# Background stages of the mixers: one at every product instead of at set distances

## The chip, the cores and the metric

The kernel runs on one core of a Trainium2 chip. The metric is the device time of one execution in microseconds (us). Three runs of the kernel before gave 865.61, 866.16 and 866.32 us; the median is 866.16 us.

## What is computed

Two layers of a streaming encoder over 256 positions of 1024 features, in float32. Cut to what matters here, a layer is:

```python
mod = cond @ ada_w[l] + ada_b[l]              # sh1, sc1, g1, sh2, sc2, g2
h = rmsnorm(x, norm1_g[l]) * (1 + sc1) + sh1
proj = h @ w_in + b_in                        # 1024 -> 6733: all q, k, v and gates
o_a = dsa_attention(...)      # 6 heads; top 64 keys of a query by an indexer of 8 heads
o_b = chunk_band_attention(...)               # 5 heads, relative bias
o_c = forgetting_attention(...)               # 5 heads, cumulated log forget gate
y = g0*(o_a @ wb_a) + g1*(o_b @ wb_b) + g2*(o_c @ wb_c)     # sigmoid gates
x = x + g1 * (y @ w_out)
h = rmsnorm(x, norm2_g[l]) * (1 + sc2) + sh2
x = x + g2 * ((silu(h @ w_g) * (h @ w_u)) @ w_ffn_out)
```

A last RMSNorm follows. A head has 64 features; softmax is taken over the 256 keys.

## The kernel before

**Products.** Every large matrix product runs in three passes: a weight is split into a rounded part `whi` (ScalarE, L187) and a rest `wlo` (VectorE, L188), the activations into `hT` of two parts, and TensorE adds hi·hi, hi·lo and lo·hi in one PSUM bank. Weights come in pieces (two blocks of 128 rows); six are held, and a piece is made when one has been used up. The 15 blocks of the input projection, the branch products and the output projection follow each other on TensorE as one stream, the *foreground*.

**Background.** All other work of the mixers is written as Python generators whose `yield` marks the end of a stage: `evac` (bias, rotary, transposes to head-major form, L560), `idx_pair` and `topk` (indexer and selection, L692 and L693 on VectorE), `forget`, and `pair`, which does two heads of an attention branch (one head for the fifth of B and C). `pair` has three stages: the scores of both heads (float32 products with 64 rows of the array each, so that two heads lie side by side: L648, L650), with VectorE taking logits and maxima (L772) and ScalarE the exponentials and the division (L776, L780); then the transposes of the weights on TensorE (L785) with their copies out of PSUM (L786); then the products with v (L792, 64 columns of the array for each of two heads, 128 for a single one). Two pairs are active at a time (`WINDOW`), so mostly four heads go through together, the *double block*; branches B, C and A follow each other. A layer has three double blocks, two single heads and one last pair.

**Order.** After each foreground product the code calls `beat(ns)`, which advances a clock by the product's nominal length (642 for six 256-column products) and then runs one stage of every generator whose time has come. The time is the clock at the last stage plus what the generator yielded: 7000 ns after the scores, 1500 after the transposes, 12000 before the rows of the gates g1 and g2 are transposed (L355, in `ada_mac`), 1500 between steps of the selection. This makes the program order. It is not the order on the engines: a list scheduler goes over the program with estimated durations and, on each engine, takes the earliest written instruction that it holds ready. Each engine then runs its own list strictly in order and waits on semaphores. PSUM has four banks for the foreground (`ps_g`) and four for the background (`ps_x`); a bank is given out again when its readers are done.

Of the kernel before, what the change touches and what calls it, by code (L numbers as in the profile page):

```python
# [94 lines left out]
def hybrid_encoder(ctx: ExitStack, tc: tile.TileContext, a):  # L95
# [105 lines left out]
    def get():  # L201
        while not ready:
            pump(1)
            if not ready:
                advance(urgent)
        got[0] += 1
        return ready.pop(0)
# [6 lines left out]

    WINDOW, LG_BUFS = 2, 4
    SKIP0, SKIP1 = 14, 22
    clock = [0.0]
    queue, active, urgent, aside = [], [], [], []  # L220

    def advance(gens):
        for e in list(gens):
            if clock[0] >= e[1]:
                try:
                    e[1] = clock[0] + next(e[0])
                except StopIteration:
                    gens.remove(e)

    def beat(ns):  # L230
        clock[0] += ns
        advance(urgent)
        advance(aside)
        while len(active) < WINDOW and queue and not (queue[0] is None and active):
            g = queue.pop(0)
            if g is not None:
                active.append([g, clock[0]])
        advance(active)
# [938 lines left out]
```

## Time and profile before

| | |
|---|---|
| median of three runs | 866.16 us |
| the profiled execution | 866.67 us, span 864.9 us |
| TensorE busy | 839.1 us (97%) |
| VectorE busy | 643.0 us (74%) |
| ScalarE busy | 473.8 us (55%) |
| granted TensorE clock | 0.997 |

The span is the time from the first to the last instruction. The mixer of the first layer takes the stretch from about 74 to 196 us, that of the second from about 470 to 606 us. In the timeline a row gives the start, the time that the row covers, engine, line, operation and count; since products overlap in the array, their cost is read from the starts of successive rows, not from their durations.

### The profile page before, as it was taken

What the parts mean: (1) busy time and instruction counts of PE and PEld (TensorE: products, weight loads), DVE (VectorE), ACT (ScalarE), POOL (GpSimd) and SP (SyncE); (2) the same over time, 40 slices, a digit from 0 to 9 for tenths busy, and PEclk for the clock granted to TensorE, in tenths of its full rate; (3) what the DMA queues carried; (4) which work ended last, traced back from release to release, by engine and by line L of the source; (5) the groups of instructions that cost most, each with busy time, mean ns of one, the idle gap of its engine ahead of it and who ended that gap; (6) DMA issues with size and microseconds to landing.
All of it is one profiled execution on the core that took longest, in us unless ns stands there. A gap on an engine that the chain in (4) does not pass through costs nothing.

```text
span 864.9 us, 14940 instructions
## 1 busy us (share of the span) xinstructions
PE 839.1 (97%) x5918; PEld 779.4 (90%) x5918; DVE 643.0 (74%) x1106; ACT 473.8 (55%) x795; POOL 51.5 (6%) x91
## 2 busy tenths in 40 slices
PE   2999999999999999999999999999999999999996
PEld 2999998999988999998889999898998899999886
DVE  6986897969987776698475786787898755647734
ACT  5556866764564544365255576767456544445521
POOL 2011210000010000000012013000000100000001
PEclk9999999999999999999999999999999999999999
DMA  9967566668846776589354456477795566636801
GB/s 353 414 251 240 186 223 225 230 232 342 316 154 274 253 273 230 184 335 380 138 194 126 142 192 240 147 280 259 272 372 194 202 222 223 218 118 255 321 14 49
DMA packets 32437, 200.48 MB, mean 232 GB/s; under 512 B 3872, under 2 KB 4144, under 8 KB 13680
## 3 DMA queue, kind: packets, MB, share of 16 engines
q1 hardware_dynamic: 30672, 194.77, 61.4%
q0 software_dynamic: 1264, 4.38, 1.6%
q8 instruction: 46, 0.75, 0.4%
q10 hardware_dynamic: 432, 0.39, 0.1%
q14 instruction: 23, 0.19, 0.1%
HBM read 198.48 MB, written 1.05 MB: 231 GB/s over the span
## 4 chain that ended last, share of the span: by engine, by line
PE 84%; DVE 9%; DMA 3%; issue 2%; ACT 2%; POOL 0%; POOLq 0%; DVEq 0%
PE ps_g L452 15%; PE ps_g L454 14%; PE ps_g L453 14%; PE ps_g L316 11%; PE ps_g L317 11%; PE ps_g L318 11%; DVE wlo L188 3%; DMA raw<-in_ada_w_dram 2%; DVE raw L340 2%; PE ps_x L650 1%; PE ps_x L454 1%; PE ps_x L452 1%; PE ps_x L453 1%; PE ps_x L792 1%; PE ps_x L648 1%
## 5 line engine op out<-in xcount | busy, mean ns | idle before, releaser
L188 DVE TENSOR_TENSOR wlo<-raw,whi 128x1024 fp32r<-128x1024 f32 (+5 forms) x300 | 333.6, 1128 | 132.6 <-ACT whi L187 131.6
L187 ACT ACTIVATE whi<-raw 128x1024 fp32r<-128x1024 f32 (+5 forms) x300 | 288.3, 975 | 248.5 <-PE ps_g L453 133.7
L452 PE MATMUL ps_g<-hT,whi 128*128 128x256 f32 x1056 | 302.2, 286 | 0.0
L454 PE MATMUL ps_g<-hT,wlo 128*128 128x256 f32 x1056 | 298.5, 283 | 0.0
L453 PE MATMUL ps_g<-hT,whi 128*128 128x256 f32 x1056 | 297.6, 282 | 0.0
L452 PEld LDWEIGHTS ps_g<-hT,whi 128*128 128x128 f32 x1056 | 199.3, 189 | 3.8 <-issue 3.7
L453 PEld LDWEIGHTS ps_g<-hT,whi 128*128 128x128 f32 x1056 | 199.5, 189 | 0.4 <-issue 0.3
L454 PEld LDWEIGHTS ps_g<-hT,wlo 128*128 128x128 f32 x1056 | 199.0, 188 | 0.3 <-issue 0.3
L340 DVE CUSTOM_DVE_ANT_0 raw<-raw,cond,adab 128x1024 f32<-128x1024 f32 x96 | 122.8, 1299 | 21.4 <-DMA raw<-in_ada_w_dram 21.2
L316 PE MATMUL ps_g<-whi,hT 128*128 128x512 f32 (+4 forms) x320 | 118.3, 372 | 1.2 <-ACT hT L1048 1.2
L317 PE MATMUL ps_g<-wlo,hT 128*128 128x512 f32 (+4 forms) x320 | 117.3, 367 | 1.8 <-DVE wlo L188 1.8
L318 PE MATMUL ps_g<-whi,hT 128*128 128x512 f32 (+4 forms) x320 | 116.6, 366 | 0.0
L316 PEld LDWEIGHTS ps_g<-whi,hT 128*128 128x128 f32 x320 | 60.5, 190 | 11.1 <-issue 2.3
L317 PEld LDWEIGHTS ps_g<-wlo,hT 128*128 128x128 f32 x320 | 60.6, 189 | 9.5 <-DVE wlo L188 2.0
L318 PEld LDWEIGHTS ps_g<-whi,hT 128*128 128x128 f32 x320 | 60.7, 190 | 7.9
L316 PE MATMUL ps_g<-whi,aT 128*128 128x512 f32 (+1 forms) x176 | 66.4, 377 | 0.0
L317 PE MATMUL ps_g<-wlo,aT 128*128 128x512 f32 (+1 forms) x176 | 66.3, 377 | 0.0
L318 PE MATMUL ps_g<-whi,aT 128*128 128x512 f32 (+1 forms) x176 | 66.2, 376 | 0.0
L380 POOL TENSOR_SCALAR var<-sq 128x1 f32<-128x1 f32 x9 | 6.2, 694 | 600.8 <-ACT xn L378 598.2
L776 ACT ACTIVATE lg<-lg,mx 128x128 f32<-128x128 f32 x64 | 28.3, 443 | 20.1 <-DVE mx L772 20.0
L316 PEld LDWEIGHTS ps_g<-whi,aT 128*128 128x128 f32 x176 | 33.1, 188 | 6.0
L318 PEld LDWEIGHTS ps_g<-whi,aT 128*128 128x128 f32 x176 | 33.1, 188 | 6.1
(212 smaller groups left out, 956.4 us busy)
## 6 DMA issues: line engine op xcount, KB each, us to landing
raw<-in_ada_w_dram SPq DMA_DIRECT2D x48, 1024.0 KB, 5.3
raw<-in_w_ffn_in_dram SPq DMA_DIRECT2D x40, 1024.0 KB, 4.9
raw<-in_w_in_dram SPq DMA_DIRECT2D x30, 1024.0 KB, 5.3
raw<-in_w_ffn_out_dram SPq DMA_DIRECT2D x20, 1024.0 KB, 6.4
raw<-in_w_branch_dram SPq DMA_DIRECT2D x12, 768.0 KB, 4.6
raw<-in_w_in_dram SPq DMA_DIRECT2D x16, 512.0 KB, 8.7
raw<-in_w_out_dram SPq DMA_DIRECT2D x8, 1024.0 KB, 6.4
raw<-in_w_in_dram SPq DMA_DIRECT2D x8, 768.0 KB, 4.6
```

The lines of the kernel that those rows point to most:

```text
L187: nc.scalar.activation(hi, r, AF.Copy)
L188: nc.vector.tensor_sub(lo, r, hi.bitcast(F32))
L316: nc.tensor.matmul(ps, lh, wh, start=start, stop=False)
L317: nc.tensor.matmul(ps, lh, wl, start=False, stop=False)
L318: nc.tensor.matmul(ps, ll, wh, start=False, stop=stop)
L340: nc.vector.tensor_tensor_reduce(out=wj, in0=wj, in1=cond, op0=OP.mult, op1=OP.add, scale=ngain[:, l, int(name[2]) - 1, k:k + 1] if name[: ...
L452: nc.tensor.matmul(ps, wh[:, c], ah, start=first, stop=False, skip_group_check=True)
L453: nc.tensor.matmul(ps, wh[:, c], al, start=False, stop=False, skip_group_check=True)
L454: nc.tensor.matmul(ps, wl[:, c], ah, start=False, stop=stop, skip_group_check=True)
L648: nc.tensor.matmul(p[:, 0:P], q[:, 0:P], k[:, 0:P], start=True, stop=True)
L650: nc.tensor.matmul(p[:, P:3 * P], q[:, P:S], k, start=True, stop=True)
L776: nc.scalar.activation(lg[:, REG[t]], lg[:, REG[t]], AF.Exp, bias=mx[:, t:t + 1], scale=-1.0, accum_out=sm[:, t:t + 1])
```

## The change

A generator's time is no longer moved on by what it yields. The delay with which a generator is started (`spawn(e, d)`, so the 7000 to 10000 before the first transposes of `evac`) stays; all later distances are gone, and each active generator runs one stage at every `beat`. The scheduler, the pools, the work itself and the loads are the same.

```diff
@@ def advance(gens):
         for e in list(gens):
             if clock[0] >= e[1]:
                 try:
-                    e[1] = clock[0] + next(e[0])
+                    next(e[0])
                 except StopIteration:
                     gens.remove(e)
```

An empty line is added above, so lines after 217 have a number one higher in the new kernel.

On TensorE, in the first layer's double block of branch B: the products with v (64x256 and 64x128; `lg` the weights of a head, `ps_x` the bank written). Before:

```order
L318 MATMUL ps_g_1200<-whi_1066,hT1_109 128x384
L792 MATMUL ps_x_1280<-lg_1086,v_vb_907 64x256
L792 MATMUL ps_x_1280<-lg_1087,v_vb_907 64x256
L792 MATMUL ps_x_1280<-lg_1086,v_vb_907 64x128
L792 MATMUL ps_x_1280<-lg_1087,v_vb_907 64x128
L792 MATMUL ps_x_1287<-lg_1112,v_vb_907 64x256
L792 MATMUL ps_x_1287<-lg_1113,v_vb_907 64x256
L792 MATMUL ps_x_1287<-lg_1112,v_vb_907 64x128
L792 MATMUL ps_x_1287<-lg_1113,v_vb_907 64x128
```

And now, at the same place (L786 the transposes of the fourth head, L649 and L651 the scores of the fifth):

```order
L786 MATMUL ps_x_1120<-ident_87,lg_1068 128x128
L793 MATMUL ps_x_1154<-lg_1041,v_vb_907 64x256
L786 MATMUL ps_x_1120<-ident_87,lg_1068 128x128 x2
L793 MATMUL ps_x_1154<-lg_1042,v_vb_907 64x256
L793 MATMUL ps_x_1154<-lg_1041,v_vb_907 64x128
L793 MATMUL ps_x_1154<-lg_1042,v_vb_907 64x128
L793 MATMUL ps_x_1161<-lg_1067,v_vb_907 64x256
L649 MATMUL ps_x_1181<-f4_0_814 128x128
L651 MATMUL ps_x_1181<-f4_0_814 128x256
L793 MATMUL ps_x_1161<-lg_1068,v_vb_907 64x256
L793 MATMUL ps_x_1161<-lg_1067,v_vb_907 64x128
L793 MATMUL ps_x_1161<-lg_1068,v_vb_907 64x128
```

The products of two heads that stood next to each other are parted by transposes and by the scores of another head.

On ScalarE, ahead of the same double block: the first softmax of the layer. Before, the forget gate (`fa`) came ahead of it, with two loads of an activation table:

```order
L721 ACT_TABLE_LOAD
L721 ACTIVATE fa_1336<-fa_1336 128x10
L187 ACTIVATE whi_1138<-raw_860 128x768
L722 ACT_TABLE_LOAD
L722 ACTIVATE fa_1336<-fa_1336 128x10
L776 ACT_TABLE_LOAD
L776 ACTIVATE lg_1086,sm_1095<-lg_1086,mx_1094 128x128
L776 ACTIVATE lg_1086,sm_1095<-lg_1086,mx_1094 128x256
```

And now:

```order
L187 ACTIVATE whi_1000<-raw_778 128x768
L187 ACTIVATE whi_1023<-raw_812 128x768
L777 ACT_TABLE_LOAD
L777 ACTIVATE lg_1041,sm_1050<-lg_1041,mx_1049 128x128
L777 ACTIVATE lg_1041,sm_1050<-lg_1041,mx_1049 128x256
L777 ACTIVATE lg_1042,sm_1059<-lg_1042,mx_1058 128x128
L781 ACTIVATE lg_1041<-lg_1041,sm_1050 128x128
L781 ACTIVATE lg_1041<-lg_1041,sm_1050 128x256
L777 ACTIVATE lg_1042,sm_1059<-lg_1042,mx_1058 128x256
```

The softmax stands ahead of the forget gate, with one table load (which here waits for the maxima of VectorE), and a head is divided as soon as its exponentials are done.

## Rows read from the trace of the kernel before

**Rows 1.** The page: busy us, share of the span and instructions of each engine.
```profile
PE 839.1 (97%) x5918; PEld 779.4 (90%) x5918; DVE 643.0 (74%) x1106; ACT 473.8 (55%) x795; POOL 51.5 (6%) x91
```

**Rows 2.** Windows of the two mixers: length, busy PE, PEld, DVE, ACT, POOL.
```profile
74.00:196.00 122.00, 120.23 (x937) 111.87 (x937) 100.50 (x254) 85.80 (x197) 10.95 (x18) 1.00 0.62 224
470.00:606.00 136.00, 135.29 (x1062) 127.32 (x1061) 101.86 (x256) 93.59 (x212) 10.07 (x16) 1.00 0.60 207
```

**Rows 3.** Timeline, TensorE: products with v of two pairs, foreground around.
```profile
146.85 0.28 PE L826 MATMUL ps_g<-oh,whi 128*128 128x256 f32 x1
146.97 0.29 PE L827 MATMUL ps_g<-oh,wlo 128*128 128x256 f32 x1
147.18 1.52 PE L792 MATMUL ps_x<-lg,v_vf 128*64 128x256 f32 x16
...
148.85 0.28 PE L453 MATMUL ps_g<-ol,whi 128*128 128x256 f32 x1
```

**Rows 4.** Timeline, TensorE: products with v of one pair.
```profile
191.55 0.28 PE L827 MATMUL ps_g<-oh,wlo 128*128 128x256 f32 x1
191.75 0.87 PE L792 MATMUL ps_x<-lg,va 128*64 128x256 f32 x8
...
192.78 0.28 PE L453 MATMUL ps_g<-ol,whi 128*128 128x256 f32 x1
```

**Rows 5.** Timeline, TensorE: scores of one pair.
```profile
178.83 0.28 PE L454 MATMUL ps_g<-hT,wlo 128*128 128x256 f32 x1
179.03 0.49 PE L648 MATMUL ps_x<-kaT,qaT 64*128 64x128 f32 x4
...
180.11 0.28 PE L453 MATMUL ps_g<-hT,whi 128*128 128x256 f32 x1
```

**Rows 6.** Timeline, TensorE: scores of a single head, foreground around.
```profile
111.83 0.34 PE L318 MATMUL ps_g<-whi,hT 128*128 128x384 f32 x1
112.10 0.48 PE L648 MATMUL ps_x<-f 64*128 64x128 f32 x2
...
113.23 0.34 PE L317 MATMUL ps_g<-wlo,hT 128*128 128x384 f32 x1
```

**Rows 7.** Timeline, TensorE: products with v in branch B, first layer.
```profile
107.93 0.34 PE L318 MATMUL ps_g<-whi,hT 128*128 128x384 f32 x1
108.93 1.99 PE L792 MATMUL ps_x<-lg,v_vb 128*64 128x256 f32 x16 [0.67 <-ACT lg L786]
...
111.13 0.34 PE L317 MATMUL ps_g<-wlo,hT 128*128 128x384 f32 x1
```

**Rows 8.** Timeline, TensorE: transposes of a gate's row and scores, second layer.
```profile
590.65 0.28 PE L454 MATMUL ps_g<-hT,wlo 128*128 128x256 f32 x1
590.77 0.60 PE L355 MATMUL ps_x<-ident,mg 128*128 128x128 f32 x4
...
592.39 0.37 PE L648 MATMUL ps_x<-kaT,qaT 64*128 64x128 f32 x1 [0.61 <-DVE ol L797]
...
593.47 0.28 PE L453 MATMUL ps_g<-hT,whi 128*128 128x256 f32 x1
```

**Rows 9.** Timeline, TensorE: groups of twelve and of three transposes.
```profile
143.85 1.47 PE L785 MATMUL ps_x<-ident,lg 128*128 128x128 f32 x12
...
158.55 0.49 PE L785 MATMUL ps_x<-ident,lg 128*128 128x128 f32 x3
```

**Rows 10.** Timeline, VectorE: first maximum of branch B, first layer.
```profile
96.77 0.27 DVE L772 CUSTOM_DVE_ANT_0 lg<-ps_x,relW 128x128 f32<-128x128 f32 x1
```

**Rows 11.** Timeline, ScalarE: table load and softmax, branch B, first layer.
```profile
97.02 1.28 ACT L776 ACT_TABLE_LOAD   x1
...
100.08 1.48 ACT L780 ACTIVATE lg<-lg,sm 128x128 f32<-128x128 f32 x4
```

**Rows 12.** Waits of ScalarE: us in total, times, longest.
```profile
ACT whi L187 <- PE ps_g L453: 133.7, 96, 4.5
```

**Rows 13.** Timeline, VectorE: last sum for the gate's row of rows 8.
```profile
562.69 0.08 DVE L340 DVE_READ_ACCUMULATOR2_ANT mg<- 128x1 f32 x1
```

## The prediction

> **What bounds the kernel now.** I read the page first: TensorE is busy 839.1 of 864.9 us, VectorE 74% [rows 1]. The reader is to see that no other engine can be the limit over the whole, and that little is left to win: about 26 us of TensorE's idle time, most of it at the start and the end, which the change does not touch. Next the windows: the change acts in the two mixers alone, 122 and 136 us long, where TensorE idles 1.8 and 0.7 us by the profile, while VectorE works 100.5 of 122 us in the first [rows 2]. Then the timeline of TensorE around each background group. A busy TensorE can hide a loss, since the ends of its products are modelled; so I measure a group from the start of the foreground product ahead of it to the start of the second product behind it, and take away two foreground products (0.12 us each at 256 columns, from the first two starts in [rows 3]; 0.175 at 384, in proportion).
>
> So measured, the products with v of two pairs cost 1.88 - 0.24 = 1.64 us [rows 3], of one pair 1.23 - 0.24 = 0.99 [rows 4]. A pair more costs 0.65; the remaining 0.34 is what it costs to go from the whole array to halves of it and back. The scores of a pair cost 1.28 - 0.24 = 1.04 [rows 5]; they have as many columns, so their own 0.65 leaves 0.39 for the two changes. A single head's scores cost 1.40 - 0.35 = 1.05 [rows 6], as much as a pair's: a head that runs without a neighbour in the other half wastes that neighbour's place. These prices, 0.17 to 0.195 per change of the array's division and 0.43 for a lone 256-column product (two thirds of 0.65), carry the forecast.
>
> Last, the waits inside groups: the products with v at 107.93 took 3.20 - 0.35 = 2.85 us against 1.64, 1.2 lost to a copy that was not done [rows 7]; the group at 590.65 took 2.82 - 0.24 = 2.58 against 0.44 for its transposes and 1.04 for its scores, 1.1 lost to a PSUM bank not yet read [rows 8]. Eight such groups of the mixers lose 0.25 us or more, 5.4 us in all; these two lose most.
>
> **The change part by part.** The instructions of TensorE, VectorE and ScalarE are the same; SP's queue is in the same order, POOL's differs by one memset. Only places change, so the sum is what TensorE loses and wins by them.
>
> *Spread transposes: nothing.* The transposes of a head now stand as one and two among foreground products, not as twelve in a row. Twelve cover 1.47 us and three 0.49 [rows 9], so nine more cost 0.98, 0.109 each, and there is no fixed price for a group.
>
> *Changes of the array's division: +4.0.* Counted in the order, they rise from 52 to 74, because transposes (whole array) and scores (row halves) now stand between the products with v (column halves). 22 by 0.18 is 4.0. Ends: 0, if TensorE would wait there anyway, and 22 by 0.39 (each costing a whole trip), 8.6. I take the rows' mean since the new changes are of the same two kinds.
>
> The Trainium skill (TensorEngine Tiling (Array Packing), Tiling Modes) says that changing the tiling mode drains the array, and (TensorE: Matmul & The Clock Gate, on the drain) that a drain is about 128 cycles, which at full clock is 0.05 us. By that estimate the 22 changes cost 1.2 and the forecast is 2.8 lower; rows 4 and 5 show more than three times as much per change, so the measured price stands.
>
> *Parted heads: +6.4.* In all six double blocks the first 256-column product with v stands alone between transposes (6 by 0.43 = 2.6). In five the third head's is parted from the fourth's as well, though a 128-column one runs beside it (5 by 0.21 = 1.1). In the two last pairs of A the heads are parted (2 by 0.43 = 0.9), and in three pairs the scores are done head by head (3 by 0.65 = 1.9). Ends: 0, and 9 if no 128-column product finds a neighbour.
>
> *Old waits: -5.4.* They go with the places where they stood; end: 0, if each returns.
>
> *New waits: +4.* Set distances were slack; now a step stands where the scheduler's estimate holds it ready. First double block of B: from the first score to the first transpose TensorE has two pairs of scores (1.30), a change (0.2), six products of 326 and six of 384 columns (1.95): 3.45 us. What it waits for: scores 0.49 [rows 5], maximum 0.27 [rows 10], the table load, which now waits for that maximum, 1.28; three exponentials (four fill 98.30 to 100.08, 0.44 each) 1.33, one copy 0.37 [rows 11]: 3.74, some 0.15 more for hand-overs. So about 0.45 late. In C the bias transposes need a bank that VectorE frees, as in a group of before that lost 0.8. Nearest rows for the rest are the old waits, 5.4 over eight, 0.67 each; six double blocks by 0.67 is 4. Ends: 0, and 12 if all twelve blocks wait as long as the worst, 1.0 to 1.2. What is queued behind a waiting transpose is the foreground itself, and all else hangs on that.
>
> The Trainium skill (ScalarE: Activation LUTs, What ACT_TABLE_LOAD costs) gives 2.66 us for a load with its drain, which would make that first wait 1.8. Here the load starts at 97.02 and the exponential runs 1.28 later [rows 11]; the trace disagrees, and 1.28 is used.
>
> *The 12000 ns before the gates' rows: nothing.* In the second layer the last sum is ready at 562.69 [rows 13] and the transposes come at 590.77 [rows 8], 28 us later; in the new order they stand about 16 us of foreground earlier, so 12 remain. If that cover went, TensorE would wait for the landing of a weight.
>
> *Feeding of weights: nothing.* ScalarE waited 133.7 us for free piece buffers [rows 12], so pieces lie ready; six of them are about 17 us of TensorE (24 products of 0.12 each). A softmax of four heads holds ScalarE and VectorE some 8 us.
>
> Sum: 866.67 (the profiled execution, span and 1.8 around it) + 4.0 + 6.4 - 5.4 + 4 = 875.7. That execution lies 0.5 above the median, so 875.2.
>
> **The rivals.**
>
> *Faster.* The finer order ends waits, and the parted products cost nothing because they fill time in which TensorE would have waited. For it: the lone product stands between the first and the other transposes of a head, where the second copy is 0.37 away. Against: there are six such places (2.2 us), and elsewhere a ready foreground product could have stood there. With 2 of the 10.4 left and no new wait: 866.2 - 5.4 + 2 = 862.8. It decides from the point where parting and new waits together stay under 3.7.
>
> *No change.* Parting at 5 to 7 us, few new waits, old waits gone: 866 to 868. For it: waits and parting partly lie on each other. It needs both terms at half.
>
> *VectorE becomes the bound.* In the first mixer it has 21.5 us of idle time [rows 2]; a softmax and the selection now come close together, and ahead of weight pieces. If the lead of 17 us is used up in two blocks, TensorE stands 4 to 6 us each time: 885. Against: rows 12, and VectorE's total does not change.
>
> **How the numbers follow.** Forecast 0.70, VectorE 0.08, no change 0.12, faster 0.10. Differences under 0.2% (1.7 us) can't be told from none here: slower 0.78, same 0.12, faster 0.10. The forecast's own range is 869 (terms of parting at half, new waits 3) to 883 (new waits 12). For 8 in 10 it goes down to 866, into the case of no change, and up to 885.
>
> **What would show it.** Right: products with v of a double block spread over 2.5 to 4 us with transposes and scores between; transposes as x1 and x2 among foreground at no cost; new small waits of TensorE on ScalarE's `lg` in the mixers; both mixer stretches longer, 4 to 6 us each; nothing changed in the feed-forward parts. Wrong: mixers of equal length, a change of the array's division at 0.05, or TensorE waiting for `wlo`. The forecast falls if parted products cost less than half of 0.43, or if the waits on `lg` add up to more than 12 us.

## The result, and the profile after

The changed kernel takes 878.18 us (median of 4 runs, 877.99 to 879.77), the kernel before 865.88 (median of 4 runs, three of them the ones told above). The recorded ratio is 1.0158, 95% interval 1.0146 to 1.0171; the two medians alone make 1.0142. Measured again later, it was 880.26 against 864.81 beside it, 1.0178 (1.0164 to 1.0192). The forecast was slower, 875.2 in a range of 866 to 885; the sign, the place and the range held, and the point was 3 us low.

The page after, first the line of the engines (its columns as in [rows 1]):

```profile
PE 850.0 (97%) x5918; PEld 780.9 (89%) x5918; DVE 642.9 (73%) x1106; ACT 476.7 (54%) x795; POOL 49.2 (6%) x91
```

The reader is to see that TensorE is busy 10.9 us longer with the same 5918 instructions, and is still at 97%. The span grew by 13.2 us, so busy time hides part of the loss, as the prediction said. VectorE works as long as before, ScalarE 2.9 us longer, GpSimd 2.3 us shorter.

Where it went: the transposes that open the next norm start at 251.87 instead of 244.91 us, 440.95 instead of 433.59, 675.87 instead of 662.49, and the profiled span is 878.1 instead of 864.9. The first and the third of these places, in the kernel before and after:

```profile
244.91 0.27 PE L397 MATMUL ps_x<-ident,xn 128*128 128x128 f32 x1
251.87 0.27 PE L398 MATMUL ps_x<-ident,xn 128*128 128x128 f32 x1
662.49 0.38 PE L397 MATMUL ps_x<-ident,xn 128*128 128x128 f32 x2
675.87 0.38 PE L398 MATMUL ps_x<-ident,xn 128*128 128x128 f32 x2
```

So the first mixer costs 7.0 us, the second 6.0 (675.87 - 662.49 less the 7.4 carried along), and the feed-forward parts next to nothing (0.4 in the first layer).

A double block's products with v after, TensorE alone, answering to [rows 3, 7]:

```profile
99.74 0.34 PE L318 MATMUL ps_g<-wlo,hT 128*128 128x384 f32 x1
99.91 0.27 PE L786 MATMUL ps_x<-ident,lg 128*128 128x128 f32 x1
100.11 0.65 PE L793 MATMUL ps_x<-lg,v_vb 128*64 128x256 f32 x2
100.69 0.44 PE L786 MATMUL ps_x<-ident,lg 128*128 128x128 f32 x2
101.06 0.87 PE L793 MATMUL ps_x<-lg,v_vb 128*64 128x256 f32 x8
101.86 0.48 PE L649 MATMUL ps_x<-f 64*128 64x128 f32 x2
102.18 0.59 PE L651 MATMUL ps_x<-f 64*128 64x256 f32 x2
102.71 0.86 PE L793 MATMUL ps_x<-lg,v_vb 128*64 128x256 f32 x6
103.50 0.44 PE L319 MATMUL ps_g<-whi,hT 128*128 128x384 f32 x1
103.78 0.34 PE L317 MATMUL ps_g<-whi,hT 128*128 128x384 f32 x1
```

The 1.99 us row of [rows 7] has become three, with transposes and the fifth head's scores between. From 99.74 to 103.78, less two foreground products (0.35), the group costs 3.69 us, and nothing in it waits. By the prices of the prediction it was to cost about 4.0: three transposes 0.33, the products of two pairs 1.30, the first head's lone product 0.43, the third head's 0.21, the fifth head's scores 0.65, six changes of division 1.08. The five other double blocks look alike.

What TensorE waits for (total, times, longest), and the slack of the weight pieces, which answers to [rows 12]:

```profile
PE ps_x L786 <- ACT lg L781: 6.8, 7, 1.8
ACT whi L187 <- PE ps_g L454: 146.8, 104, 4.5
```

(Lines are one higher than before: L781 is the division of the softmax, L786 the transposes.) The first row is new: seven times TensorE stands at the first transposes of a head because that division isn't done. In the second row ScalarE still waits for free piece buffers, 146.8 us against 133.7, so the feeding of weights is no bound.

The first of these waits, around the first double block of branch B (VectorE, ScalarE and TensorE), answers to [rows 10, 11]:

```profile
88.50 0.28 DVE L694 MATCH_REPLACE8 sc<-m,sc 128x128 f32<-128x128 f32 x1
88.89 0.96 DVE L188 TENSOR_TENSOR wlo<-raw,whi 128x768 fp32r<-128x768 f32 x1
89.77 0.28 DVE L773 CUSTOM_DVE_ANT_0 lg<-ps_x,relW 128x128 f32<-128x128 f32 x1
90.14 1.28 ACT L777 ACT_TABLE_LOAD   x1 [2.43 <-DVE mx L773]
...
91.04 0.34 PE L319 MATMUL ps_g<-whi,hT 128*128 128x384 f32 x1
...
93.15 0.33 PE L786 MATMUL ps_x<-ident,lg 128*128 128x128 f32 x1 [1.76 <-ACT lg L781]
```

The scores begin at 87.64. The maximum comes 2.13 us later, since VectorE first does steps of the selection and a weight's `wlo`; then comes the table load; and TensorE, done with its foreground product of 91.04, starts the transpose at 93.15. By groups this wait is 2.05 us.

In branch A the cause is VectorE's queue alone (the same at 587.51 in the second layer):

```profile
163.27 2.35 DVE L188 TENSOR_TENSOR wlo<-raw,whi 128x1024 fp32r<-128x1024 f32 x2
165.54 0.29 DVE L773 CUSTOM_DVE_ANT_0 lg<-ps_x,sc 128x128 f32<-128x128 f32 x1
...
168.07 0.33 PE L786 MATMUL ps_x<-ident,lg 128*128 128x128 f32 x1 [0.93 <-ACT lg L781]
```

And in branch C ScalarE's:

```profile
115.88 1.06 ACT L187 ACTIVATE whi<-raw 128x1024 fp32r<-128x1024 f32 x1 [2.76 <-PE ps_g L319]
116.96 1.28 ACT L777 ACT_TABLE_LOAD   x1
...
119.97 0.33 PE L786 MATMUL ps_x<-ident,lg 128*128 128x128 f32 x1 [1.46 <-ACT lg L781]
```

Summed over eleven groups with 0.3 us or more, by what each costs above its own products, TensorE now waits 10.0 us in the mixers: 2.05 (91.04), 1.78 (118.07), 1.31 (590.96), 1.15 (166.86), 1.1 (107.30), and six of 0.3 to 0.64. Before it was 5.4.

About 1.0 of these 10.0 us is not waiting but TensorE's clock. Behind the wait that ends at 93.15, the granted clock is 0.50, which is 1.2 GHz, from 93.65 to 97.06 us. The foreground products of 384 columns then start 0.32 us apart (94.31, 94.62, 94.94, 95.27) instead of 0.175, and three of the six small items lie there (93.23, 95.58, 96.44). In the second trace of the same kernel, that of the later measurement, the same wait (1.76 us) leaves the clock at 1.00, and the three come to 0.2 us. Two windows, the first run and the second (columns as in [rows 2]; the third number from the end is the clock):

```profile
94.00:97.00 3.00, 3.00 (x12) 2.81 (x12) 2.84 (x17) 2.97 (x11) 0.59 (x2) 0.50 0.19 47
95.00:98.00 3.00, 3.00 (x21) 2.79 (x21) 2.79 (x18) 2.97 (x12) 0.86 (x2) 1.00 0.14 26
```

In the second trace the clock is at 0.50 from 22.95 to 26.37 instead, behind a wait of 1.8 us ahead of the mixers, and in the kernel before from 23.27 to 26.68. Over a stretch in which only one of the two traces of the changed kernel has the low clock, that trace loses 1.5 us against the other. Each has one such stretch, so both spans are 878.1, and the second trace, with the stretch where the kernel before has it, reaches the first of the norms above at 251.85: the 7.0 us of the first mixer are not the clock's.

### The profile page after: what moved, and what is told of

It is laid out like the page before. It is cut to its first block, busy times and chain, and to the rows that moved or that the text cites. A ratio compares the mean times of both kernels' runs of the same rounds, so it can differ in the third digit from the quotient of the medians.

```text
span 878.1 us, 14936 instructions
## 1 busy us (share of the span) xinstructions
PE 850.0 (97%) x5918; PEld 780.9 (89%) x5918; DVE 642.9 (73%) x1106; ACT 476.7 (54%) x795; POOL 49.2 (6%) x91
## 4 chain that ended last, share of the span: by engine, by line
PE 90%; ACT 4%; DVE 3%; issue 1%; DMA 1%; POOLq 0%; POOL 0%; ACTq 0%; DVEq 0%
PE ps_g L453 15%; PE ps_g L455 15%; PE ps_g L454 15%; PE ps_g L318 11%; PE ps_g L317 11%; PE ps_g L319 11%; PE ps_x L793 2%; PE ps_x L786 2%; DVE wlo L188 1%; PE ps_x L398 1%; PE ps_x L651 1%; ACT lg L777 1%; PE ps_x L453 1%; PE ps_x L454 1%; PE ps_x L455 1%
## 5 line engine op out<-in xcount | busy, mean ns | idle before, releaser
L187 ACT ACTIVATE whi<-raw 128x1024 fp32r<-128x1024 f32 (+5 forms) x300 | 288.4, 975 | 247.4 <-PE ps_g L454 146.8
L317 PE MATMUL ps_g<-whi,hT 128*128 128x512 f32 (+4 forms) x320 | 119.3, 375 | 0.9 <-ACT hT L1049 0.9
L319 PE MATMUL ps_g<-whi,hT 128*128 128x512 f32 (+4 forms) x320 | 118.4, 372 | 0.0
L318 PEld LDWEIGHTS ps_g<-wlo,aT 128*128 128x128 f32 x176 | 33.1, 188 | 5.9
```

Source lines behind the costliest of these rows:

```text
L187: nc.scalar.activation(hi, r, AF.Copy)
L317: nc.tensor.matmul(ps, lh, wh, start=start, stop=False)
L318: nc.tensor.matmul(ps, lh, wl, start=False, stop=False)
L319: nc.tensor.matmul(ps, ll, wh, start=False, stop=stop)
```

## The experiments

The theory: two costs that add up. One is parting, since products of the array's halves are cut up by work on the whole array or on its row halves; the other is waiting, since the first transposes stand where the scheduler's estimate, not the engines, holds the weights ready.

Where an experiment adds lines to the kernel, the line numbers in its rows are up to three higher than in the kernel that it starts from.

**Which distance, and which cost.** Three kernels take the pair's two distances apart.

Only the 7000 ns after the scores act again in the changed kernel:

```diff
-                    next(e[0])
+                    d = next(e[0])
+                    if d < 0:
+                        e[1] = clock[0] - d
...
-            yield 7000
+            yield -7000
```

> The new kernel with one distance back: 7000 ns after the scores of a pair; all others stay gone. In its order the array's division changes 52 times, as in the kernel before, and no product with v is parted from its neighbour. Theory (the loss is parted products with v, some 7.5 us, and waits of the transposes for the softmax, some 9 against 3 to 5 before): both go, 866 us (864.5 to 868). Rival (the other distances, of selection, indexer, forget gate and the gates' rows, carry a good part of the loss): 869 to 873.

Measured: 867.41 against 865.46 of before, 1.0022 (1.0013 to 1.0031). The array's division changes 52 times as before. The waits on `lg` ahead of the transposes are gone, and others came:

```profile
PE ps_x L358 <- DVE mg L343: 1.6, 2, 1.1
PE ps_x L795 <- ACT lg L789: 1.3, 1, 1.3
```

The first row is the transposes of the gates' rows, which now have no 12000 ns ahead of them.

Only a distance before the products with v acts again, 7000 instead of 1500, so that they stay together while the transposes stay early (with the same lines in `advance` as above):

```diff
...
-            yield 1500
+            yield -7000
```

> The new kernel with one distance back: 7000 ns between the transposes and the products with v; the transposes still come at the first product after the scores. In its order transposes stand spread and early as in the new kernel (117 background groups), but the products with v stand together again (52 changes of the array's division). Theory (two costs that add): the parting goes, the waits for the softmax stay, 870.7 us (869.5 to 872.5). Rival 1 (only the waits cost; the parted products fill time in which TensorE would wait): 877 to 879. Rival 2 (only the parting costs; new waits merely stand for old ones): 865 to 867.

Measured: 869.6, 1.0044 (1.0031 to 1.0056). The division changes 52 times, a double block is one row again (1.52 us at 104.48), and the waits on `lg` come to the same sum as in the changed kernel (6.8):

```profile
PE ps_x L788 <- ACT lg L783: 6.6, 6, 2.6
```

This is the run that separates the two costs. By the medians 878.2 - 869.6 = 8.6 us go to parting and 869.6 - 865.5 = 4.1 to waits, old ones already set off. The profiles, which both have the clock at 0.50 around the first wait or behind it (here from 94.02 to 97.44), put parting a little higher: with this order the norms behind the mixers start at 246.85, 435.47 and 665.81 us, so of the changed kernel's mixers 5.0 and 4.6 us are gone (251.87 - 246.85, and 234.92 - 230.34 between the two later marks), 9.6 together. So parting is 8.6 to 9.6 us and the rest 3.1 to 4.1, and that rest may hold part of what the low clock costs.

In the kernel before, only the pair's two distances are taken away:

```diff
-            yield 7000
+            yield 0
...
-            yield 1500
+            yield 0
```

> The kernel before with the two distances of a pair (7000 after the scores, 1500 ahead of the products with v) set to 0; all other distances stay. In its order the array's division changes 71 times (52 before, 74 in the new kernel). Theory: nearly the whole loss, 876.5 us (874.5 to 878.5). Rival (the other distances carry a good part): 867 to 872.

Measured: 880.1, 1.0173 (1.0158 to 1.0188), with 71 changes of division and 7.8 us of waits on `lg`. That is 1.6 us above the range that was expected; in its profile the clock is at 0.50 twice in the mixers, from 99.57 to 102.98 and from 516.00 to 519.41 us, behind waits of 3.3 and 2.0 us. The whole loss comes from these two numbers.

The counterpart: in the changed kernel both act again, and all other distances stay away (the diff is that of the first kernel, at both places).

> The changed kernel, but the two distances of the attention heads (7000 after the scores, 1500 before the products with v) act again; every other distance stays away. It is the counterpart of the run in which only these two were taken away. Theory (these two carry the whole loss; the others cost at most what the gates' rows wait): the array's division changes 52 times as before, the waits on the weights lg are gone, 1 to 2 us of waits appear at the rows of the gates, and the time is 866.5, between 865.5 and 868, against 865.5 of before. Rival (the other distances do harm of their own that the first run hid): above 869.

Measured: 865.57 against 864.81 of the runs beside it, 1.0011 (1.0002 to 1.002), as the theory had it: 52 changes, and TensorE's waits in the mixers are these and smaller ones:

```profile
PE ps_x L358 <- DVE mg L343: 1.8, 2, 1.3
PE ps_x L730 <- DVE fl L727: 0.6, 1, 0.6
PE ps_x L788 <- ACT lg L783: 0.3, 1, 0.3
```

**The price of parting.** First, whether the order alone parts two heads: in the kernel before, each head's products with v stand together, not in turns with its neighbour's.

```diff
-            for kt in range(T):
-                for i, h in enumerate(hs):
+            for i, h in enumerate(hs):
+                for kt in range(T):
```

> The kernel before, with all distances, but the products with v of a pair written head by head (256 and 128 columns of the one, then of the other), so that the wide product of the second head has only the narrow one of the first beside it. Nothing else in TensorE's order moves. Theory (a lone product costs its full length): six double blocks by 0.64 and two last pairs by 0.43 are 4.7, so 870.6 us (869.5 to 871.6). Rival (a lone product costs little, since the division's change or the feed sets the pace): 866 to 867.5.

Measured: 865.12, 1.0001 (0.9991 to 1.0011): the theory's 870.6 failed, the rival was right. The group, which in [rows 3] cost 1.64:

```profile
145.15 0.28 PE L827 MATMUL ps_g<-oh,wlo 128*128 128x256 f32 x1
145.36 1.57 PE L792 MATMUL ps_x<-lg,v_vf 128*64 128x256 f32 x16
...
147.09 0.28 PE L453 MATMUL ps_g<-ol,whi 128*128 128x256 f32 x1
```

1.94 - 0.24 = 1.70. If every product started only behind all those written ahead of it in either half, 128- and 256-column products would leave one half empty in turns; they don't. In these runs only work on another division of the array parts heads.

So two kernels put such work there, in the kernel before: a transpose of a constant for each of the 14 pairs of heads, once ahead of the pair, once between the first and the second head's first products. The second leaves out a right sum for these pairs, since its transpose comes into their bank in the middle of the sum; only its times are read. (Both also pass `skip_group_check=True` to the products with v.)

```diff
             po = ps_x()
             n = P // len(hs)
+            if len(hs) == 2:
+                nc.tensor.transpose(po[:, 256:384], ident, ident)
...
```

And between, behind the product in the loop over `kt` and `i`:

```diff
...
+                    if len(hs) == 2 and kt == 0 and i == 0:
+                        nc.tensor.transpose(po[:, 256:384], ident, ident)
```

> The kernel before with the same 14 transposes, but ahead of each pair's products with v, whose heads stay together; where two pairs follow each other (six double blocks) the second transpose parts the pairs, with two changes of the array's division more and no lone product. Theory: 14 by 0.11 and 12 changes by 0.18 are 3.7, 869.2 us (868 to 870.5). With a change at 0.05 us: 2.1, 867.6. The difference to the kernel with the transpose between the heads is 16 changes and 14 lone products: 8.9 by theory.

> The kernel before, all distances kept, with one transpose of a constant into unused columns put between the wide products with v of the two heads of each of the 14 pairs. Per pair one transpose (0.11), two changes of the array's division more (0.36) and one lone wide product (0.43). Theory: 14 by 0.9 is 12.6, 878 us (875 to 880). Rival 1 (a change costs a drain of 0.05 us): 1.5 + 1.4 + 6 is 8.9, 874. Rival 2 (a lone product costs nothing, as when heads were written one after the other): 1.5 + 5.0 is 6.5, 872.

Measured: ahead 867.12 against 865.13, 1.0022 (1.0011 to 1.0032); between 872.12, 1.0083 (1.0064 to 1.0102). A double block with the transposes ahead:

```profile
145.23 0.28 PE L830 MATMUL ps_g<-oh,wlo 128*128 128x256 f32 x1
145.36 0.27 PE L791 MATMUL ps_x<-ident 128*128 128x128 f32 x1
145.56 0.87 PE L794 MATMUL ps_x<-lg,v_vf 128*64 128x256 f32 x8
146.36 0.33 PE L791 MATMUL ps_x<-ident 128*128 128x128 f32 x1
146.62 0.87 PE L794 MATMUL ps_x<-lg,v_vf 128*64 128x256 f32 x8
...
147.64 0.28 PE L453 MATMUL ps_g<-ol,whi 128*128 128x256 f32 x1
```

2.41 - 0.24 = 2.17 us, 0.53 above [rows 3]. Two transposes are 0.22, so the two changes that the second one adds cost 0.31, about 0.15 each. The time alone would say less: it rose by 2.0, less than expected, and 14 transposes by 0.11 leave 0.04 for each of 12 changes. The rows tell why. Four of the six double blocks cost about 0.53 more, but the two of branch B only 0.32 and 0.31 more (106.16 and 516.09), since their products waited before, and the group of [rows 8] loses 0.45 less here; with 0.11 for each last pair that makes 2.5, inside the measured interval (0.9 to 2.8).

The last pair of A, with the transpose between the heads, answers to [rows 4]:

```profile
194.38 0.28 PE L830 MATMUL ps_g<-oh,wlo 128*128 128x256 f32 x1
194.59 0.65 PE L792 MATMUL ps_x<-lg,va 128*64 128x256 f32 x2
195.17 0.33 PE L796 MATMUL ps_x<-ident 128*128 128x128 f32 x1
195.43 0.86 PE L792 MATMUL ps_x<-lg,va 128*64 128x256 f32 x6
...
196.45 0.28 PE L453 MATMUL ps_g<-ol,whi 128*128 128x256 f32 x1
```

2.07 - 0.24 = 1.83. With the transpose ahead of it the same pair costs 1.11 (190.47 to 191.82). Parting it costs 0.72: two changes, 0.31, and 0.41 for the lone product, against the 0.43 that the prediction took. The time of 872.12 is not the theory's 878 but the one expected if a lone product cost nothing; the rows show another reason for it. A double block with both pairs parted costs 2.89 (147.60 to 150.73), and 2.89 - 2.17 is 0.72 again, not twice that: in the second parting one head's product runs beside the other pair's 128-column ones, and its lone product costs nothing. The two times were expected to differ by 8.9, with a lone product in each of the 14 pairs; only eight are lone (one in each of six double blocks, and the two last pairs). Eight by 0.72 are 5.8; the medians differ by 5.0, the profiled spans by 7.1 (871.9 and 864.8), of which 1.4 are longer waits elsewhere.

**What the waits hang on.** An exponential was put ahead, to have the activation table loaded before the first maximum. At first its input was a constant:

```diff
+                early = small.tile([P, 1], F32, name="early", bufs=1)
+                nc.scalar.activation(early, neghalf, AF.Exp)
```

> The new kernel with one more exponential of 128 values on ScalarE early in each mixer, so that the table of the exponentials is loaded long before the first softmax. TensorE's order stays. Theory (the first wait of the new kernel, 2.05 us at 91.04, holds a table load of 1.28 us that waits for the maxima): that wait falls to about 0.8, in the second layer 0.5 may go: 876.6 us (876 to 877.2). Rival (VectorE's late maxima set that wait, the load lies beside them): 878.

Measured: 881.33 against 865.13, 1.019 (1.0169 to 1.021). This run says nothing about the load: the scheduler put the exponential at 2.53 us, at the program's start, and the load in front of the first softmax stayed (1.28 us at 89.90). Its time is above both forecasts; the changed kernel was not run beside it. With a column of `v_vb` as input, written ahead of the first scores of B:

```diff
+            if br == 1 and hs[0] == 0:
+                early = small.tile([P, 1], F32, name="early", bufs=1)
+                nc.scalar.activation(early, v[:, 0, 0:1], AF.Exp)
```

> The changed kernel with an exponential of one column of v_vb written ahead of the scores of the first pair of branch B, so that the activation table is loaded before the first maximum instead of behind it. Rival (the load itself is the cause of the 2.05 us wait ahead of the first transposes): the wait falls by the load's 1.28 to about 0.8, the time by 1.3 to about 877 in each layer where that load stands there. Theory (a step stands where the scheduler's estimate holds it ready, so a cause that the estimate knows is taken back by an earlier place): the first transposes stand five products of 384 columns earlier, 0.175 each, 0.9 in all, so the wait falls only to about 1.65 and the time stays within 1 us of the changed kernel beside it.

Measured: 885.53 against 864.81 of before, 1.0238 (1.0224 to 1.0253); the changed kernel beside it was at 880.26 (its expectation stands below). The load is out of the way, and the wait is longer:

```profile
78.86 1.28 ACT L770 ACT_TABLE_LOAD   x1
...
90.12 0.34 PE L317 MATMUL ps_g<-whi,hT 128*128 128x384 f32 x1
90.60 0.40 ACT L780 ACTIVATE lg<-lg,mx 128x128 f32<-128x128 f32 x1 [2.94 <-DVE mx L776]
...
92.82 0.48 PE L789 MATMUL ps_x<-ident,lg 128*128 128x128 f32 x1 [2.36 <-ACT lg L784]
```

The first exponential begins 0.83 us earlier than in the changed kernel (90.60, not 91.43), the first transpose 0.33 earlier (92.82 for 93.15); but TensorE arrives there 0.92 earlier (its last product starts at 90.12, not 91.04). In the new order the first transposes stand five products of 384 columns earlier: what the load's place saved is given back, and more. The rival, that the load alone is the cause of the wait, falls: without it in the chain TensorE still waits 2.36 us. What stays is VectorE's lateness: the first exponential still waits for a maximum. That the estimate misses just this is argued from these rows, not shown by a run of its own. The time rose more than the theory allowed, by 5.3 us; the loads of the forget gate and of the softmax now stand one behind the other in front of the fifth head (2.5 us of waiting at 106.4, in the changed kernel 1.1). And the clock is at 0.50 twice in the first mixer, from 92.32 to 95.73 and from 109.38 to 112.80 us, where the second trace of the changed kernel has it once, ahead of the mixers; at 1.5 us a stretch, as measured above, that is an estimated 1.5 us more. The rest stays open.

> The changed kernel once more, word for word, so that the runs beside it have it on the same chip. 878.2 us as measured, between 877 and 880; by the theory the sum of parted products (about 8.6) and waits (about 4) is a property of the order and doesn't vary with the chip. Theory and rival give the same here.

Measured: 880.26, just above this range.

Last, in the kernel before, a longer distance ahead of the products with v, against the wait at 107.93 [rows 7]:

```diff
-            yield 1500
+            yield 4000
```

> The kernel before with 4000 instead of 1500 ns between the transposes of a pair and its products with v. Theory (some of TensorE's waits of the kernel before, 1.2 us in branch B of the first layer and 0.5 in the second, are products with v that come before the copies are done): those go, 864.3 us (863.5 to 865.5). Rival (other waits of the same size take their place, a bank of PSUM or a row later): 865.5 to 867.

Measured: 868.18 against 865.13, 1.0028 (1.0016 to 1.004), slower, and above what theory and rival had. The old wait is gone; in its place come others, and around the longest of them, which ends at 136.95, the clock is at 0.50 from 135.48 to 142.31 us:

```profile
PE ps_x L741 <- DVE lg L744: 2.5, 2, 2.1
PE ps_x L648 <- DVE oh L799: 1.5, 2, 0.9
```

```profile
137.00:142.00 5.00, 5.00 (x23) 4.13 (x24) 3.73 (x21) 3.55 (x14) 0.00 (x0) 0.50 0.56 216
```

From 136.95 on TensorE worked 5.4 us at 1.2 GHz, which by an estimate is 2.7 us lost, most of the 3.05 by which the time rose. Of the twelve executions the four with a mean granted clock of 0.996 to 0.998 took 866.0 to 866.7 us, the eight with 0.993 to 0.995 took 867.3 to 869.3.

No version that was run beats the kernel before by more than can be told apart.

## Why the prediction was right, and which terms were not

The direction was right for the reason given: the two additive costs exist, they lie on TensorE's path, and both follow from the pair's two distances alone. Against the forecast of +9.0 the change cost 12.3 and 15.4 us by the medians of the two measurements. Of the signs, a double block's products cover about 3.7 to 4.6 us (2.5 to 4 was said) and the mixers are 7.0 and 6.0 us longer (4 to 6 was said). By terms:

- *Spread transposes: nothing.* Held. In the changed kernel, at full clock, most single transposes that don't wait cost 0.11 to 0.12, most pairs 0.22.
- *Changes of the division: +4.0.* Nearly held: 22 by the measured 0.15 is 3.3. The Trainium skill (TensorEngine Tiling (Array Packing), Tiling Modes) says that a change of the mode drains the array. The trace agrees that a change costs time; the 0.05 that the prediction estimated from the Trainium skill's drain figure (TensorE: Matmul & The Clock Gate, Step-by-step: what each phase is for) is a third of what the rows show.
- *Parted heads: +6.4.* A little too large. 8.6 measured for all of parting (by the medians) leaves 8.6 - 3.3 = 5.3, which is 6.4 - 1.1; by the profiles' 9.6 it is 6.3. The price of a lone product (0.43, measured 0.41) was right; the count was wrong. The third head's product (5 by 0.21 = 1.1) runs beside 128-column products and costs nothing, as the doubly parted block shows. In the changed kernel the five double blocks in which it is parted are 0.26 to 0.31 cheaper than worked out by the prediction's prices, the one in which it isn't (544.90) only 0.03. That the total came within 3 us is in part luck: this count was too high where the next term was too low.
- *Old waits -5.4 and new waits +4.* This is the step that failed, by 4.5 to 5.5 us: -1.4 was forecast, +3.1 to +4.1 measured. The old waits did go, but the new ones are 10.0, not 4, or about 9 without the clock. The worked example shows the mistake. It gave 0.45 us for the first block; 2.05 came. The links behind the maximum were right, the load's 1.28 too. The Trainium skill (ScalarE: Activation LUTs, What ACT_TABLE_LOAD costs) gives 2.66 us for a load with its drain; in the trace the first exponential starts 1.29 us behind the load's start (90.14 and 91.43), so it disagrees here too. The first link was wrong: 0.49 from the scores to the first maximum, as if VectorE stood ready. It took 2.13, because VectorE's queue had selection steps and a `wlo` in front, 1.64 more; and 0.45 + 1.64 = 2.09. In the kernel before, the maximum of [rows 10] also starts 2.40 us behind its first score (94.37), so the number was there to be read. Of the four other large waits two have a pair of `wlo`, 2.35 us, in front, the other two a table load.
- *The 12000 ns: nothing.* Held in the changed kernel, where no row of a gate waits; but the cover depends on the order around it. In the two kernels that hold the pair back and let the gates' rows go early, these rows wait 1.6 and 1.8 us.
- *Feeding of weights: nothing.* Held.
- *TensorE's clock: no term.* The prediction has none. A long wait can be followed by a stretch at 1.2 GHz, which cost 1.5 us where two traces of one kernel could be compared, and 2.7 by an estimate in the kernel with the longer distance.

Of the rivals, *faster* needed parting to cost nothing or 2 us; it costs 8.6 or more. *No change* needed both terms at half. *VectorE the bound* did not come by its mechanism (TensorE never waits for `wlo` in the mixers), though VectorE's queue is behind three of the five large waits (91.04, 166.86, 590.96) in another way: weight pieces that nobody needs yet stand ahead of maxima that TensorE needs.

What stays open: whether the two ratios of the changed kernel, 1.0158 and 1.0178, differ at all, since their intervals overlap; why the clock fell behind some waits and not behind others of the same length; and what of the 5.3 us of the early exponential comes from the order further on.

## What to carry to other kernels

A distance that reads like slack may be what keeps a helper's stages whole: here it kept products on halves of the array side by side, and without it 8.6 to 9.6 us went into the same products with transposes between. Before pricing a wait by the durations of its chain, look at what stands in the queue of the first engine of the chain, since a step that is placed by an estimate is, as the rows here suggest, late by what the estimate leaves out there. Taking away one cause of a wait can gain nothing: in the one run that tried it, the consumer moved forward. And look at the granted clock behind a long wait before a slower time is put down to the wait alone.

## What the runs showed of the hardware

Products on the two column halves fill each other even when each head's stand together in the order (group 1.70 us for 1.64, time 1.0001), so here the halves need not be written in turns. A transpose between two column-half products of a pair costs 0.72 us where nothing else runs beside the lone product, 0.31 of it the two changes of division. In a block with two partings only one lone product is paid for, since the other runs beside the next pair's products: 2.89 us against 2.17 for a block with its transposes ahead, 0.72 apart once and not twice. After a wait of 1.76 us TensorE's granted clock was 0.50 (1.2 GHz) from 93.65 to 97.06 us in one trace of the changed kernel and stayed at 1.00 in the other, which was 1.5 us of difference there.
